# One layer of a hybrid encoder in one program: operands of the 512-column matmuls laid 256 bytes apart modulo 512 in SBUF

## The chip, the cores and the metric

The kernel runs on one core of one Trainium2 chip, as one program in one launch. The metric is device time in microseconds (us); the time before is the median of three runs, 946.27 us. The engines are named as in the profile: PE is TensorE's matmuls and PEld its loads of weights, DVE is VectorE, ACT is ScalarE, POOL is GpSimd and SP is SyncE, whose queue issues most of the DMAs. In this text a matmul's *stationary* operand is the one that PEld loads, and its *moving* operand the one that PE streams through; `pe.matmul(dst, a, b)` has `a` stationary and `b` moving. The *distance* of two operands is the difference of their byte addresses within a partition of SBUF, taken modulo 512.

## What is computed

One layer over 512 tokens of 1024 channels, in float32: a recurrent branch A and an attention branch B, merged by gates, and then a feed-forward block with a causal convolution. Both halves are normalised before and after.

```python
h = rms_norm(x, mix_norm_pre)
xa, ga, q, k, v, f, gA, gB = split(h @ w_in)
xc  = causal_conv4(xa)
y_a = gelu(ga) * rg_lru(xc, w_rg_a, w_rg_x, ...)      # 1280 channels
y_b = forgetting_attention(q, k, v, f + b_forget)     # 16 heads of 64
m   = sigmoid(gA) * (y_a @ w_proj_a) + sigmoid(gB) * (y_b @ w_proj_b)
x   = x + rms_norm(m @ w_out, mix_norm_post)
h   = rms_norm(x, ffn_norm_pre)
u   = causal_conv3(h @ w_up)                           # 6144 channels
x   = x + rms_norm((gelu(u_gate) * u_val) @ w_down, ffn_norm_post)
```

## The kernel before

**Three matmuls for one.** Each product is taken in three, to keep float32's precision in a faster format: an operand is split into a high part and a remainder (`hi` by ACT, `lo` by DVE; a tile of weights becomes `wh` and `wl`, activations `hh` and `hl`, `yh` and `yl`, `mh` and `ml`, `ah` and `al`), and `mm3` (L221) adds high by high, high by low and low by high into one bank of PSUM. `project` (L226) does that over the 8 blocks of 128 channels of k: 24 matmuls for one tile of 128 output channels by 512 tokens, each with its own load of 128 x 128 weights.

**The stages**, in the order in which TensorE runs them:

- xa: 10 tiles with the weights stationary and hh, hl moving. The first four (the *head*) run in halves of 256 tokens (`half`, L455): 192 matmuls of 256 columns. The other six, 144 matmuls of 512 columns, alternate with the recurrent gates (`gate_mm`, L371), whose stationary operand is `gh` or `gl` and whose moving one is xh, xl or a *halo* tile copied from the neighbours: 96 of 512 columns.
- v: 2 x 4 units; here hh, hl are stationary and the weights move (`v_mm`, L300): 192.
- ga: 10 tiles (240), then pa: 8 tiles over 10 blocks of k with yh, yl moving (240), and between them f, 16 small ones.
- The attention loop: for each of 8 pairs of heads q, k and ma by `project` (24 each), scores, the transposes `pt` of the probabilities P against `ident`, and `av`. Then mb and pb, 8 tiles each; in pb yb moves. So q, k, ma and mb have 768 matmuls of 512 columns together, pb 192.
- wo: mh, ml stationary, the weights moving (`out_matmuls`, L834): 192.
- up: the up-projection, all in matmuls of 256 columns with the weights stationary. Three pairs of tiles run plainly, in two halves of tokens (288); 21 pairs run in seven products of 12 (`Pair.product`, L901): 84 a pair, 1764 together. The remainders `ml` of some of their weights are made by an accumulating DMA on POOL's queue (L875).
- dn: the down-projection, 42 steps of 12 matmuls (`down_step`, L1198) with `ah`, `al` stationary and the weights moving: 504 of 512 columns. The `ah`, `al` of the first six steps lie in the pool `ff`, those of the others in `down`.

**Weights** come through one pool, `weights`, with tags `raw`, `wh` and `wl` of four buffers of 4096 bytes each. `unit` (L215) has them fetched two tiles ahead: a DMA on SP's queue into `raw`, ACT's copy to `wh`, DVE's subtraction to `wl`.

**Where tiles lie.** Pools are stacked from the left end of SBUF upwards or, with `side="right"`, from the right end downwards, in the order in which they are opened and closed; within a pool the tags follow one another in the order of their first use, each size rounded up to 32 bytes per partition. `offset(stack, n, side)` (L85) opens a pool of `n` bytes that nothing uses, so that what is opened behind it shifts by `n`. From the left there stand, in the kernel before: `consts` (a tile of 480 bytes that nothing uses, then 1952 bytes), `weights`, `small` (29 slots of 32 bytes), 160 bytes, hT (hh and hl), 320 bytes, vy0; on them `xc`, 448 bytes and `rgw` for the gates, later vy1, pa, tg and attn; and after these have gone, 96 bytes, x2, `norm` or `ff`, `up`, and at the end 256 bytes and `down`. From the right: 32 bytes; then 128 bytes and `rgate`; later h2T, 128 bytes and `merged`; and, when that is closed, `sums`, `tsum`, 448 bytes and `strassen`. The weights begin at 0 modulo 512, h2T at 448.

Of the kernel before, what the change touches and what calls it, by code (L numbers as in the profile page):

```python
# [8 lines left out]
F32 = mybir.dt.float32  # L9
# [7 lines left out]
P = 128  # L17
# [46 lines left out]
def kernel(  # L64
# [20 lines left out]
    def offset(stack, n, side="left"):  # L85

        places[0] += 1
        pool = stack.enter_context(tc.tile_pool(name=f"offset{places[0]}", bufs=1, side=side))
        pool.tile([P, n // 4], F32, name=f"offset{places[0]}")

    cpool = ctx.enter_context(tc.tile_pool(name="consts", bufs=1))
    cpool.tile([P, 120], F32, name="offset0")
    offset(ctx, 32, "right")
    wpool = ctx.enter_context(tc.tile_pool(name="weights", bufs=4))
    pstk = ctx.enter_context(ExitStack())
    pspools = [pstk.enter_context(tc.tile_pool(name="psum", bufs=8, space=PSUM, reuse_waits="tile"))]
    small = ctx.enter_context(tc.tile_pool(name="small", bufs=4))

    def bank(name):
        return pspools[-1].tile([P, 512], F32, tag="ps", name=name)  # L100
# [114 lines left out]
    def unit(name, ahead=2):  # L215

        i = where[name]
        fetch(i + ahead)
        return ready.pop(name)
# [6 lines left out]
    def project(dst, unit, ah, al, lo=0, hi=S):  # L226
        wh, wl = unit
        for k in range(KD):
            mm3(dst[:, lo:hi], wh[:, k], wl[:, k], ah[:, k, lo:hi], al[:, k, lo:hi], k == 0, k == KD - 1)
# [51 lines left out]

    mstk = ExitStack()
    gstk = ExitStack()
    offset(mstk, 160)
    hpool = mstk.enter_context(tc.tile_pool(name="hT", bufs=1))
    hh = hpool.tile([P, KD, S], F32R, name="hh")
    hl = hpool.tile([P, KD, S], F32R, name="hl")
    offset(mstk, 320)
    vpools = [mstk.enter_context(tc.tile_pool(name="vy0", bufs=4, reuse_waits="tile"))]
    vt, yb = {}, {}  # L290
    sp4 = cpool.tile([P, TR], F32, name="sp4")
# [27 lines left out]
    with ExitStack() as rg:  # L319
        rt, ixt, tt = {}, {}, {}  # L320
        last_act = [None]
        with ExitStack() as r0:
            xpool = r0.enter_context(tc.tile_pool(name="xc", bufs=6, reuse_waits="tile"))
            offset(r0, 448)
            gwpool = r0.enter_context(tc.tile_pool(name="rgw", bufs=2, reuse_waits="tile"))
            xc, xh, xl = {}, {}, {}

# [17 lines left out]
            def gate_prep(t):  # L345
                n = HROWS[t]
                raw = gwpool.tile([P, 4, P], F32, tag="graw", name=f"graw{t}")
                gh = gwpool.tile([P, 4, P], F32R, tag="gh", name=f"gh{t}")
                gl = gwpool.tile([P, 4, P], F32R, tag="gl", name=f"gl{t}")
                nc.sync.dma_start(raw, rgw[:, t])  # L350
                act.copy(gh, raw)
                stacked = 3 * n <= P
                hw = slice(0, 2 if stacked else 4)
                dve.tensor_tensor(out=gl[:, hw], in0=raw[:, hw], in1=gh[:, hw].bitcast(F32), op=ALU.subtract)
                th = gwpool.tile([P, S], F32R, tag="halo_h", name=f"halo_h{t}")
                tl = None
                if stacked:
                    q = slice(2 * n, 3 * n)
                    dve.tensor_tensor(out=gh[q, 2:4], in0=raw[q, 2:4], in1=gh[q, 2:4].bitcast(F32), op=ALU.subtract)
                    dsts = ((th, 0, xh), (th, n, xl), (th, 2 * n, xh))  # L360
                else:
                    tl = gwpool.tile([P, S], F32R, tag="halo_l", name=f"halo_l{t}", bufs=1)
                    dsts = ((th, 0, xh), (tl, 0, xl))
                for dst, o, src in dsts:
                    for c0, c1 in HALO[t]:
                        i = c0 // P
                        nc.sync.dma_start(dst[o : o + c1 - c0].bitcast(F32), src[i][c0 - i * P : c1 - i * P].bitcast(F32))
                        o += c1 - c0
                gw[t] = gh, gl, th, tl
# [22 lines left out]
            with tc.tile_pool(name="pre", bufs=2, side="right", reuse_waits="tile") as pre:  # L392
# [131 lines left out]
                split_a(2)  # L524
                fetch(NF + 1)
                gate_prep(0)
                conv_a(3, pss[3])
                split_a(3)

            offset(rg, 128, "right")  # L530
            rpool = rg.enter_context(tc.tile_pool(name="rgate", bufs=TR, side="right", reuse_waits="tile"))
            for t in range(NF, TR + NF):
                u = unit(order[t][0])
# [132 lines left out]
    def gate_tile(e, which):  # L666
        c = 0 if which == "ma" else KD
        pg = bank(f"{which}{e}")
        project(pg, unit(f"{which}{e}"), hh, hl)
        tg = tgpool.tile([P, S], F32, tag="tg", name=f"tg_{which}{e}")  # L670
        act.activation(out=tg, in_=pg, func=AF.Tanh, scale=0.5, bias=hb[:, c + e : c + e + 1])
        return tg

    with ExitStack() as at:
        apool = at.enter_context(tc.tile_pool(name="attn", bufs=2, reuse_waits="tile"))
# [8 lines left out]
        def prep_alloc(p):  # L684
            bias = []
            for h in (2 * p, 2 * p + 1):
                B = apool.tile([P, PO[NT]], F32, tag="B", name=f"B{h}")
                nc.gpsimd.dma_start(B, cnd[h : h + 1, :].partition_broadcast(P))
                for c0, w, o in ((0, 256, 0), (256, 512, 384)):
                    diag = B[:, c0 : c0 + 2 * w].rearrange("p (a b) -> p a b", a=2)[:, :, o : o + P]  # L690
                    nc.gpsimd.dma_start(diag, mask2, accum_op=ALU.add)  # L691
                bias.append(B)
            return bias

        def halves(ps, name):
            hi = apool.tile([P, S], F32R, tag=f"{name[0]}h", name=f"h_{name}")
            lo = apool.tile([P, S], F32R, tag=f"{name[0]}l", name=f"l_{name}")
            act.copy(hi, ps)
            dve.tensor_tensor(out=lo, in0=ps, in1=hi.bitcast(F32), op=ALU.subtract)
            return hi, lo  # L700
# [30 lines left out]
        def normalise(pts):  # L731
            for Pt, sm in pts:
                dve.reciprocal(sm, sm)
                for b in (3, 2, 0, 1):
                    w = P * (b + 1)
                    dve.tensor_scalar(out=Pt[:, PO[b] : PO[b] + w], in0=Pt[:, PO[b] : PO[b] + w],
                                      scalar1=sm[:, b : b + 1], scalar2=None, op0=ALU.mult)
# [45 lines left out]
        for p in range(KD):  # L783
            bias = prep_alloc(p)
            pq, pk = bank(f"q{p}"), bank(f"k{p}")
            project(pq, unit(f"q{p}"), hh, hl)
            if prev is not None:
                normalise(prev)
            project(pk, unit(f"k{p}"), hh, hl)
            q = halves(pq, f"q{p}")  # L790
            k = halves(pk, f"k{p}")
            if prev is not None:
                pts = pt(p - 1, prev)
            tg = gate_tile(p, "ma")
            dve.scalar_tensor_tensor(out=pa[:, p], in0=tg, scalar=1.0, in1=pa[:, p], op0=ALU.add, op1=ALU.mult)
            if prev is not None:
                av(p - 1, pts)
            prev = scores(p, q, k, bias)
# [8 lines left out]
    h2pool = ustk.enter_context(tc.tile_pool(name="h2T", bufs=1, side="right", reuse_waits="tile"))  # L807
    h2h = h2pool.tile([P, KD, S], F32R, name="h2h")
    h2l = h2pool.tile([P, KD, S], F32R, name="h2l")
    offset(gstk, 128, "right")  # L810
    mgpool = gstk.enter_context(tc.tile_pool(name="merged", bufs=1, side="right", reuse_waits="tile"))
    mh = mgpool.tile([P, KD, S], F32R, name="mh")
    ml = mgpool.tile([P, KD, S], F32R, name="ml")
# [13 lines left out]
    mstk.close()  # L827

    fstk = ctx.enter_context(ExitStack())
    offset(fstk, 96)  # L830
    xpool = fstk.enter_context(tc.tile_pool(name="x2", bufs=1, reuse_waits="tile"))
    x2t = xpool.tile([P, NT, D], F32, name="x2t")
    nc.sync.dma_start(x2t, xv)
# [100 lines left out]
    with ExitStack() as mix:  # L934
# [112 lines left out]
        for ps, u in first:  # L1047
            project(ps, u, h2h, h2l, 256, S)

    ypool = fstk.enter_context(tc.tile_pool(name="ff", bufs=3, reuse_waits="tile"))  # L1050
    ydram = ctx.enter_context(tc.tile_pool(name="ffd", bufs=1, space=bass.MemoryType.DRAM))
    yd = [ydram.tile([P, 2, S], F32, name=f"yd{j}") for j in range(JF // 2)]
# [86 lines left out]
    p, n = pairs[NU], pairs[NU + 1]  # L1139
# [85 lines left out]
    with man2:  # L1225
# [3 lines left out]
        b, p = pairs.pop(JF - 2), pairs.pop(JF - 1)  # L1229
# [45 lines left out]
        gelu(p.g)  # L1275
        glu(p.j, p.g, p.v)
        ustk.close()
        offset(fstk, 256)
        dpool = fstk.enter_context(tc.tile_pool(name="down", bufs=1, reuse_waits="tile"))
        dpools.append(dpool)  # L1280
        q = {}
# [207 lines left out]
```

## Time and profile before

| what | value |
|---|---|
| three runs | 944.2, 946.27, 946.84 us |
| profiled execution, span from the first to the last instruction | 941.1 us |
| granted clock of TensorE, mean | 0.998 |
| transposes `pt` of the attention loop | 256 by 226 ns, busy 10.7 us |
| DMA | 182.29 MB, mean 194 GB/s |
| POOL's `ml<-raw_up`, 512 KB | 20 DMAs, 5.5 us from issue to landing |

The profile is of one execution, apart from the timed runs; of it only the span is known, and the runs' median lies 5.2 us above that, for what comes ahead of the first instruction and behind the last. In the views of the profile a row of the windows gives, for a stretch of time, how long an engine was busy and how many of its instructions lie in the stretch in whole or in part. The duration of a matmul is longer than the time from its start to the start of the next, since matmuls are pipelined: rates are read from starts, or from counts over a stretch. The chain of waits follows the work that ended last back from the end; the view of the waits names, for each engine and line, what released it and how long it had stood.

### The profile page before, as it was taken

Reading aid. Unit: us, or ns where it says so; the run is one execution under the profiler, and the core shown is the slowest. Engines: PE = TensorE matmul, PEld = TensorE weight load, DVE = VectorE, ACT = ScalarE, POOL = GpSimd, SP = SyncE. Lnnn points to the kernel's source line nnn. Section 1 sums busy time; section 2 is a strip of 40 time slices with the busy share of each in tenths; the row PEclk is TensorE's granted clock in tenths of the full one; section 3 lists DMA queues with packets and bytes.
Section 4 is the critical chain, followed back from the end, with each engine's and each line's share of the span. In section 5 each row is a group of like instructions: output and inputs, shape, how many; then the busy total and the mean of one; then the engine's idle time right before and its main releaser. Section 6 shows DMA issues by size and latency. Waiting matters only on the chain.

```text
span 941.1 us, 14954 instructions
## 1 busy us (share of the span) xinstructions
PE 924.7 (98%) x5582; PEld 801.3 (85%) x5582; DVE 687.5 (73%) x1121; ACT 570.3 (61%) x982; POOL 228.6 (24%) x240
## 2 busy tenths in 40 slices
PE   9999999999999999999999999999999999999996
PEld 7888888887888888888888879999999999978885
DVE  5866369533757777777544488998888898889897
ACT  7554495333346666565322486687777878677664
POOL 4134335444243222220111000042322323100001
PEclk9999999999999999999999999999999999999999
DMA  7667589989686555552123753287898998799764
GB/s 276 227 212 209 155 224 277 248 194 254 174 227 151 152 151 149 157 154 70 68 90 103 282 187 123 57 233 184 201 214 211 207 219 207 217 367 335 235 207 143
DMA packets 76282, 182.29 MB, mean 194 GB/s; under 512 B 7281, under 2 KB 35745, under 8 KB 75826
## 3 DMA queue, kind: packets, MB, share of 16 engines
q1 hardware_dynamic: 45056, 123.13, 39.2%
q0 software_dynamic: 30864, 57.68, 29.9%
q8 instruction: 44, 0.72, 0.3%
q10 hardware_dynamic: 290, 0.53, 0.1%
q14 instruction: 28, 0.23, 0.1%
HBM read 148.59 MB, written 33.64 MB: 194 GB/s over the span
## 4 chain that ended last, share of the span: by engine, by line
PE 88%; DMA 5%; DVE 3%; ACT 2%; issue 1%; SPq 0%; DVEq 0%; ACTq 0%
PE up L915 5%; PE up L912 5%; PE up L913 5%; PE dn L1212 4%; PE dn L1210 4%; PE dn L1211 4%; DMA ml<-raw_up 4%; PE pa L224 2%; PE ga L224 2%; PE ga L223 2%; PE pa L223 2%; PE pa L222 2%; PE ga L222 2%; PE q L222 2%; PE ma L222 2%; PE wo L840 2%
## 5 line engine op out<-in xcount | busy, mean ns | idle before, releaser
L875 POOL DMA_DIRECT2D ml<-raw_up x41 | 36.5, 889 | 199.3 <-DVE ml L847 77.4
L1065 DVE SCALAR_TENSOR_TENSOR u<-up,cpt,u 128x511 f32<-128x511 f32 x96 | 71.3, 745 | 2.6 <-ACT u L1059 0.9
L1212 PE MATMUL dn<-wh_dn,al 128*128 128x512 f32 x168 | 65.6, 390 | 0.8 <-DVE al L847 0.8
L1210 PE MATMUL dn<-wh_dn,ah 128*128 128x512 f32 x168 | 65.4, 389 | 0.0
L1211 PE MATMUL dn<-wl_dn,ah 128*128 128x512 f32 x168 | 65.4, 389 | 0.0
L912 PE MATMUL up<-sh,th 128*128 128x256 f32 x252 | 61.8, 280 | 0.3 <-ACT x L919 0.3
L913 PE MATMUL up<-sl,th 128*128 128x256 f32 x252 | 61.6, 279 | 0.0
L175 DVE TENSOR_TENSOR wl_dn<-raw_dn,wh_dn 128x1024 fp32r<-128x1024 f32 x42 | 51.5, 1226 | 9.1 <-ACT wh_dn L172 8.9
L172 ACT CAST wh_dn<-raw_dn 128x1024 fp32r<-128x1024 f32 x42 | 44.1, 1050 | 17.3 <-issue 11.5
L847 DVE TENSOR_TENSOR tl<-t,th 128x1024 fp32r<-128x1024 f32 x42 | 51.1, 1217 | 1.8 <-ACT th L893 1.8
L1059 ACT ACTIVATE u<-up,cpt 128x512 f32<-128x512 f32 x48 | 37.0, 779 | 21.6 <-PE up L915 12.3
L893 ACT CAST th<-t 128x1024 fp32r<-128x1024 f32 x42 | 44.0, 1047 | 8.8 <-DVE t L847 6.1
L912 PEld LDWEIGHTS up<-sh,th 128*128 128x128 f32 x252 | 47.5, 188 | 0.7 <-ACT x L919 0.5
L913 PEld LDWEIGHTS up<-sl,th 128*128 128x128 f32 x252 | 47.5, 189 | 0.0
L691 POOL DMA_DIRECT2D B<-maskf x32 | 39.1, 1751 | 28.6 <-DMA B<-cnd 24.2
L1073 POOL TENSOR_TENSOR yf<-u,u 128x512 f32<-128x512 f32 x24 | 32.7, 1379 | 39.1 <-ACT u L1069 21.4
L912 PE MATMUL up<-h2h,mh 128*128 128x256 f32 x168 | 41.0, 279 | 0.0
L913 PE MATMUL up<-h2l,mh 128*128 128x256 f32 x168 | 41.0, 279 | 0.0
L931 DVE TENSOR_TENSOR up<-up,x 128x256 f32<-128x256 f32 x63 | 27.0, 432 | 17.9 <-PE up L915 9.4
L915 PE MATMUL up<-sh,tl 128*128 128x256 f32 x252 | 39.6, 279 | 0.0
L1212 PEld LDWEIGHTS dn<-wh_dn,al 128*128 128x128 f32 x168 | 31.5, 188 | 8.2 <-DVE al L847 1.6
L175 DVE TENSOR_TENSOR wl_pa<-raw_pa,wh_pa 128x640 fp32r<-128x640 f32 x16 | 13.1, 818 | 34.1 <-ACT wh_pa L172 34.1
(654 smaller groups left out, 3183.0 us busy)
## 6 DMA issues: line engine op xcount, KB each, us to landing
raw_up<-in_w_up_dram SPq DMA_DIRECT2D x48, 512.0 KB, 6.0
td<-in_w_down_dram POOLq DMA_DIRECT2D x36, 512.0 KB, 6.0
raw_dn<-td SPq DMA_DIRECT2D x24, 512.0 KB, 4.8
B<-cnd POOLq DMA_DIRECT2D x16, 640.0 KB, 5.2
ml<-raw_up POOLq DMA_DIRECT2D x20, 512.0 KB, 5.5
raw_dn<-in_w_down_dram SPq DMA_DIRECT2D x18, 512.0 KB, 4.2
raw_wo<-in_w_out_dram SPq DMA_DIRECT2D x16, 512.0 KB, 3.8
td<-td POOLq DMA_DIRECT2D x12, 512.0 KB, 10.7
```

Of the source, the lines that this page charges most:

```text
L172: act.copy(self.wh, self.raw)
L175: engine.tensor_tensor(out=self.wl, in0=self.raw, in1=self.wh.bitcast(F32), op=ALU.subtract)
L222: pe.matmul(dst, ah, bh, start=first, stop=False)
L847: dve.tensor_tensor(out=out, in0=a, in1=b, op=ALU.subtract)
L893: act.copy(self.th[i], self.t[i])
L912: pe.matmul(dst, wh[:, k], ah[:, k], start=first and k == 0, stop=False, skip_group_check=True)
L913: pe.matmul(dst, wh[:, k], al[:, k], start=False, stop=False, skip_group_check=True)
L915: pe.matmul(dst, wl[:, k], ah[:, k], start=False, stop=k == KH - 1, skip_group_check=True)
L1065: dve.scalar_tensor_tensor(out=c[:, s:], in0=ps[:, : S - s], scalar=col(C_CFW + 3 * e + j), in1=c[:, s:], op0=ALU.mult, op1=ALU.add)
L1210: pe.matmul(dst[t], ah[:, k, tok], wh[:, k], start=first, stop=False, skip_group_check=True)
L1211: pe.matmul(dst[t], ah[:, k, tok], wl[:, k], start=False, stop=False, skip_group_check=True)
L1212: pe.matmul(dst[t], al[:, k, tok], wh[:, k], start=False, stop=last, skip_group_check=True)
```

## The change

Only the places of tiles change: the sizes and the order of the tiles that are not used, and the place of the pool `small` ahead of the weights instead of behind them. Every instruction stays, in its order.

```diff
     cpool = ctx.enter_context(tc.tile_pool(name="consts", bufs=1))
-    cpool.tile([P, 120], F32, name="offset0")
     offset(ctx, 32, "right")
+    small = ctx.enter_context(tc.tile_pool(name="small", bufs=4))
+    offset(ctx, 64)
     wpool = ctx.enter_context(tc.tile_pool(name="weights", bufs=4))
     pstk = ctx.enter_context(ExitStack())
     pspools = [pstk.enter_context(tc.tile_pool(name="psum", bufs=8, space=PSUM, reuse_waits="tile"))]
-    small = ctx.enter_context(tc.tile_pool(name="small", bufs=4))
...
-    offset(mstk, 160)
+    offset(mstk, 256)
     hpool = mstk.enter_context(tc.tile_pool(name="hT", bufs=1))
     hh = hpool.tile([P, KD, S], F32R, name="hh")
     hl = hpool.tile([P, KD, S], F32R, name="hl")
-    offset(mstk, 320)
...
-            offset(r0, 448)
+            offset(r0, 256)
             gwpool = r0.enter_context(tc.tile_pool(name="rgw", bufs=2, reuse_waits="tile"))
...
+                if t == 0:
+                    gwpool.tile([P, 64], F32, name="offset_halo", bufs=1)
                 th = gwpool.tile([P, S], F32R, tag="halo_h", name=f"halo_h{t}")
...
-            offset(rg, 128, "right")
+            offset(rg, 192, "right")
             rpool = rg.enter_context(tc.tile_pool(name="rgate", bufs=TR, side="right", reuse_waits="tile"))
...
             q = halves(pq, f"q{p}")
+            if p == 0:
+                apool.tile([P, 64], F32, name="offset_k", bufs=1)
             k = halves(pk, f"k{p}")
...
-    offset(gstk, 128, "right")
+    offset(gstk, 192, "right")
     mgpool = gstk.enter_context(tc.tile_pool(name="merged", bufs=1, side="right", reuse_waits="tile"))
...
-    offset(fstk, 96)
     xpool = fstk.enter_context(tc.tile_pool(name="x2", bufs=1, reuse_waits="tile"))
...
+    offset(fstk, 256)
     ypool = fstk.enter_context(tc.tile_pool(name="ff", bufs=3, reuse_waits="tile"))
...
         ustk.close()
-        offset(fstk, 256)
         dpool = fstk.enter_context(tc.tile_pool(name="down", bufs=1, reuse_waits="tile"))
```

## The prediction

> **What bounds the kernel now.** The page comes first: the span, the busy times, the granted clock and the chain that ended last.
>
> ```profile
> span 941.1 us, 14954 instructions
> ## 1 busy us (share of the span) xinstructions
> PE 924.7 (98%) x5582; PEld 801.3 (85%) x5582; DVE 687.5 (73%) x1121; ACT 570.3 (61%) x982; POOL 228.6 (24%) x240
> ...
> PEclk9999999999999999999999999999999999999999
> ...
> PE 88%; DMA 5%; DVE 3%; ACT 2%; issue 1%; SPq 0%; DVEq 0%; ACTq 0%
> ```
>
> TensorE is busy for 98% of the span at full clock, and 88% of the chain is its own work. The view of the waits, for TensorE alone, says how little it is held up:
>
> ```profile
> PE up L915 <- DMA ml<-raw_up: 5.3, 6, 1.3
> PE xa L417 <- POOL ident masks.py:199: 1.5, 1, 1.5
> ```
>
> The longest sum is 5.3 us in six waits, all in the up-projection. So the time is the number of matmuls times the **spacing** of their starts, and a change of placement can act only through that spacing. The durations of the groups (some 390 ns for 512 columns) are no use here: matmuls overlap. I read the spacing from the view of windows instead. Each window below begins 0.20 us (0.06 us for 256 columns) after the start of one matmul and ends as long after the start of a later one of the same stage. With 512 columns one matmul is in flight at the left edge, so a row counting x has x-1 spacings; with 256 columns two are, so x-2. Columns: stretch, length, PE busy (count), clock, DMA share, GB/s.
>
> ```profile
> 25.16:30.81 5.65, 5.65 (x50) 1.00 0.31 100
> 112.22:131.81 19.59, 19.59 (x85) 1.00 0.51 142
> 150.26:188.94 38.68, 38.68 (x170) 1.00 1.07 257
> 194.20:223.96 29.76, 29.76 (x131) 1.00 1.04 221
> 258.10:267.48 9.38, 9.38 (x42) 1.00 0.92 256
> 460.18:467.39 7.21, 7.21 (x32) 1.00 0.30 98
> 526.27:549.83 23.56, 23.56 (x102) 1.00 0.62 216
> 668.09:676.25 8.16, 8.16 (x74) 1.00 0.90 222
> 718.51:816.03 97.52, 97.52 (x830) 1.00 0.89 215
> 823.86:829.07 5.21, 5.21 (x24) 1.00 0.98 322
> 838.08:877.75 39.67, 39.67 (x176) 1.00 0.96 339
> ```
>
> Every row is busy from edge to edge at clock 1.00, so nothing but the matmuls themselves sets these spacings. Beside each I put the distance of the stationary operand's address from the moving one's, modulo 512, worked out from the sizes of the pools in their order. The weights' tiles stand at 0 modulo 512. `small` is 29 slots of 32 bytes (928), plus 160 of offset, so hh and hl stand at 64; 320 more puts vy0, vy1, pa, tg and attn at 384. From the right, h2T stands at 448, and rgate and merged 128 lower at 320; `down` stands at 256, and the first six steps' `ah`, `al` in `ff` at 0.
>
> - v (row 112): stationary hh 64, moving weights 0: **64**; 19.59/84 = 233.2 ns
> - wo (526): stationary mh 320, moving weights 0: **320**; 23.56/101 = 233.3 ns
> - ga (150) and k, ma (258): weights 0, moving hh 64: **448**; 38.68/169 = 228.9 and 9.38/41 = 228.8 ns
> - pa (194): weights 0, moving yh 320: **192**; 29.76/130 = 228.9 ns
> - pb (460): weights 0, moving yb 384: **128**; 7.21/31 = 232.6 ns
> - dn (823): stationary ah 0, weights 0: **0**; 5.21/23 = 226.5 ns
> - dn (838): stationary ah 256, weights 0: **256**; 39.67/175 = 226.7 ns
>
> What the reader is to see: 64 and 320 agree, 448 and 192 agree, 0 and 256 agree, in stages that share nothing else (weights stationary in one, moving in the other; DMA share from 0.30 to 1.07). The spacing follows the distance modulo 256, and zero modulo 256 is the quickest shown. The 256-column rows are another matter: the head of xa (25.16, distance 448) has 5.65/48 = 117.7 ns, while the up-projection (64 throughout) has both 8.16/72 = 113.3 ns and 97.52/828 = 117.8 ns. It keeps a pattern over long stretches, and the chain of waits in order of time (start, length) shows what lies between some of them:
>
> ```profile
> 588.30:614.00 25.70, 25.70 (x220) 1.00 0.32 73
> 616.00:623.50 7.50, 7.41 (x63) 1.00 0.99 224
> 635.50:645.50 10.00, 9.00 (x80) 1.00 0.78 201
> 646.50:666.20 19.70, 19.18 (x163) 1.00 0.83 207
> 668.09:686.50 18.41, 17.62 (x156) 1.00 0.86 209
> 688.00:716.60 28.60, 27.45 (x243) 1.00 0.89 211
> 718.51:818.00 99.49, 99.49 (x840) 1.00 0.88 212
> ```
>
> ```profile
> 637.35 8.23 DMA ml<-raw_up
> ...
> 657.40 8.94 DMA ml<-raw_up
> ...
> 678.07 8.50 DMA ml<-raw_up
> ...
> 708.35 8.37 DMA ml<-raw_up
> ```
>
> Busy time by count is about 117.7 in the first, second, fourth and last stretch, about 113 in the others. The four transfers end at 645.6, 666.3, 686.6 and 716.7, where TensorE takes up again: it comes back slow, fast, fast and slow. So which pattern follows a wait is drawn there, and holds to the next.
>
> **The change, part by part.** No instruction is added, removed or moved; the tiles it adds (`offset_halo`, `offset_k`) are never touched. So all of it is distances. The new ones: `consts` loses 480 bytes and `small` moves ahead of the weights; 64 more brings the weights to 0 again. hT then starts 256 up, and with the 320 gone vy0, vy1, pa, tg and attn stand at 256 too. On the right 192 in place of 128 puts rgate and merged at 448-192 = 256. rgw starts at 0, its halo tiles at 256; `offset_k` leaves q at 256 and puts k, P and PTh at 0; `ff` and `down` stand at 256. So xa, v, ga, pa, q, k, ma, mb, pb, wo, gates, av and dn are all at 256, as the change says. f is not (its stationary slices step by 192 bytes), but has 16 matmuls. h2T and `sums` stay at 448 and their weights at 0: 64, as before.
>
> Counts are from the loops (8 blocks of k by 3 products a tile, 8 or 10 tiles). Savings, down to 226.7:
>
> - v, 192 by 233.2-226.7 = 6.5 ns: 1.25 us
> - wo, 192 by 6.6: 1.27 us
> - pb, 192 by 5.9: 1.13 us
> - ga and pa, 480 by 2.2: 1.06 us
> - q, k, ma, mb, 768 by 2.2: 1.69 us
> - xa after its head and the gates, 240 by 2.2: 0.53 us. Part of the gates (the halos) stands at zero already, and yet the stretch below, six matmuls from a halo to a halo, has 1.38/6 = 230 ns. I take it that a run of three does not settle; with distances equal throughout the stage the runs no longer break.
>
> ```profile
> 51.57:52.95 1.38, 1.38 (x7) 1.00 0.54 119
> ```
>
> - dn and av: 0 or 256 before, 256 after: nothing.
>
> That is 6.9 us. The **head of xa**, 192 matmuls of 256 columns, goes from 448 to 256, for which no row with 256 columns stands. Its bounds are 113.3 and 117.8 ns, the two patterns shown: 0.9 us to nothing. The 512-column row at the same distance is at its quickest, but v and the up-projection at 64 show that the two widths need not agree; I take the middle, 0.4 us.
>
> The **transposes** shift too: their stationary P goes from 288 to 384 (modulo 512) away from ident, which moves by 32 bytes. The groups by shape:
>
> ```profile
> L748 PE MATMUL pt<-ident,P 64*128 64x64 f32 x256 | 10.7, 226 | 0.0
> ...
> L257 PE MATMUL tr_f<-ident,xn 64*128 64x64 f32 x64 | 2.8, 229 | 0.0
> ```
>
> tr_f stands at 416, not 288, and has the same mean (229 and 226 ns): I cost them at nothing, 0.3 us either way.
>
> The **up-projection** keeps its distance, but its pattern is drawn anew after each wait, and every start ahead of it shifts. Slow in the rows above are 220+63+163+840 = 1286 of 2052 matmuls (288 and 21 pairs by 84). At 117.8-113.3 = 4.5 ns, all fast would be 5.8 us less; the other 766 at most all turned slow would be 3.4 us more. I take no change, with both ends for the range.
>
> Sum: 6.9 + 0.4 = 7.3 us, off a profiled span of 941.1: 933.8. The runs' median, 946.27, lies 5.2 us above that span for what is around it, so **939.0 us**. What TensorE gains in a stage it keeps, since the other engines follow it there, unless its weights come late. They do not now: a ga transfer lands in 5.2 us against 24 matmuls by 228.9 ns = 5.5 us a tile, two tiles are fetched ahead, and SP's queue waits there for a buffer that DVE frees, not for data.
>
> ```profile
> raw_ga<-in_w_in_dram SPq DMA_DIRECT2D x10, 512.0 KB, 5.2
> ```
>
> ```profile
> SPq L166 <- DVE wl_ga L175: 48.8, 10, 7.0
> ```
>
> If the cover went in ga and pa (DMA shares of 1.07 and 1.04), their 1.06 us would stay: 940.1.
>
> [...]
>
> **The rivals.**
>
> 1. *The up-projection settles in the slow pattern throughout.* For it: two of the four waits shown ended in it, the last, with 840 matmuls behind it, among them. Against: the fast one came back twice. 7.3 less 3.4 saved: 942.4.
> 2. *The change doesn't do what it says: placement is not the cause.* Then the two reads don't disturb each other, the spacings belong to the stages, and 512 columns stay as they are: 946.3. Against: three pairs of unlike stages agree by distance. [...]
> 3. *Slower: weights-stationary stages do not share dn's spacing.* Both rows at zero modulo 256 are dn, with an activation stationary and the weights moving. Direction does matter: 64 gives 233, and its negative 448 gives 229. If xa, gates, ga, pa, q, k, ma and mb (1488 matmuls) fell to 233.3 at 256, they would lose 1488 by 4.4 = 6.5 us, against 3.65 won in v, wo and pb: 949.2. It decides from 228.9 + 3650/1488 = 231.4 ns. Against: 256 is its own negative modulo 512, so the swap of roles leaves the distance as in dn.
>
> **How the numbers follow.** A measurement of this kernel tells from no change about 0.3%, 2.8 us, so "faster" means under 943.4. Forecast (226.7 ns at 512 columns, the up-projection mixed): 0.73. Rival 1: 0.14. Rival 2: 0.07. Rival 3: 0.04. The last 0.02 is a mishap of the new overlaps of tiles at a change of pools, worth a microsecond or two. Faster takes the forecast, rival 1 and a little: 0.88; same 0.08; slower 0.04. The range goes from 939.0-0.5 (head) less 5 of the 5.8 us of an all-fast up-projection, 933.5, to rival 1 with an unmoved head, 942.4+0.4 and 0.3 for the transposes: 943.1.
>
> **What would show it.** Right: windows over v, wo, pb, ga, pa and the attention's projections all at 226.7 ns, dn unchanged, PE's waits as before, and the rest of the difference in the stretches of the up-projection at 113.3 or 117.8. Wrong: a stage at 256 with another spacing than dn (rival 3, or 2 if it kept its old one); new waits of TensorE on a weight's DMA; an up-projection spacing outside the two patterns.

## The result and the profile after

The changed kernel takes 936.98 us in the median of 20 runs (932.72 to 942.19). The kernel before takes 943.5 us (939.87 to 948.82) in 20 runs, the three of the table above among them. The ratio is 0.9939, with a 95% interval of 0.9923 to 0.9954: 0.6% faster, twice the 0.3% that a measurement of this kernel can tell from no change. The profiled execution spans 934.0 us; its own time is 936.06, 2.1 us more. One later execution of the changed kernel took 4186 us, for a reason that was not looked into; it counts in the median of its experiment and in no ratio or mean.

From the page of the changed kernel (span, busy times, share of the chain):

```profile
span 934.0 us, 14955 instructions
...
PE 917.3 (98%) x5582; PEld 800.2 (86%) x5582; DVE 686.5 (74%) x1121; ACT 570.6 (61%) x982; POOL 230.2 (25%) x240
...
PE 91%; DMA 4%; DVE 2%; ACT 1%; issue 0%; DVEq 0%; POOL 0%; ACTq 0%; POOLq 0%
```

TensorE has the same 5582 matmuls in 7.4 us less. The windows over the changed kernel, laid as in the prediction (each begins 0.20 us after the start of a matmul and ends 0.20 us after that of a later one; 0.06 us for 256 columns; the spacing is the length divided by the count less one, or less two for 256 columns):

```profile
119.32:129.74 10.42, 10.42 (x47) 1.00 0.67 161
135.64:189.36 53.72, 53.72 (x238) 1.00 1.04 272
190.04:220.18 30.14, 30.14 (x134) 1.00 1.02 216
248.14:263.78 15.64, 15.64 (x70) 1.00 0.71 219
451.64:515.10 63.46, 63.46 (x281) 1.00 0.31 103
516.92:549.33 32.41, 32.41 (x144) 1.00 0.65 229
835.02:870.16 35.14, 35.14 (x156) 1.00 0.96 332
...
19.99:27.18 7.19, 7.19 (x62) 1.00 0.62 219
690.07:730.65 40.58, 40.58 (x360) 1.00 0.85 210
747.55:807.62 60.07, 60.07 (x512) 1.00 0.87 221
```

The first seven rows are v, ga, pa, the first pair's q, k and ma, the second phase's pb and mb, wo, and dn. They give 226.5, 226.7, 226.6, 226.7, 226.6, 226.6 and 226.7 ns: each of these 512-column stages now has dn's spacing, whichever operand stands still and whether the DMA share is 0.31 or 1.04. The eighth row, the head of xa, has 7.19/60 = 119.8 ns where it had 117.7: with 256 columns the new distance is *slower*. The last two are the up-projection, in its quick pattern (40.58/358 = 113.4 ns) and its slow one (60.07/510 = 117.8 ns), both still there.

The view of TensorE's waits:

```profile
PE up L917 <- DMA ml<-raw_up: 6.4, 6, 2.0
PE xa L418 <- POOL ident masks.py:199: 1.5, 1, 1.5
PE dn L1215 <- DVE al L849: 0.8, 1, 0.8
```

Only the first differs in a way that matters: 6.4 us for 5.3. Its longest wait, 2.0 us at 626, has an aftermath. From the timeline of TensorE, and then from the windows around it:

```profile
628.32 0.92 PE L917 MATMUL up<-h2h,ml 128*128 128x256 f32 x4 [2.02 <-DMA ml<-raw_up]
```

```profile
622.50:626.00 3.50, 3.50 (x32) 1.00 1.03 255
626.10:628.20 2.10, 0.20 (x2) 1.00 0.83 178
628.40:631.90 3.50, 3.50 (x18) 0.54 0.43 62
632.20:640.00 7.80, 7.80 (x71) 1.00 0.89 244
```

For 3.5 us after the wait the granted clock is 0.54, and 18 matmuls stand where 32 stood just before. At some 206 ns instead of 115, the 17 spacings cost another 1.5 us. A wait of 2 us here costs 3.5.

Where the 7.1 us between the two spans come from, by the start times of equal matmuls in the two traces: 0.8 us have been gained by the gates at 42 us (TensorE's waits there for xn, hl and a halo, of 0.2, 0.3 and 0.4 us, stand in the profile of before alone; it will turn out to be chance), 6.7 more by the end of wo, 0.5 in the up-projection (250.8 to 250.3 us), and 0.9 are lost after it (120.8 to 121.7 us).

### The profile page after: what moved, and what is told of

It reads as the page before. It is cut to its first block, busy times and chain, and to the rows that moved or that the text cites. A ratio compares the mean times of both kernels' runs of the same rounds, so it can differ in the third digit from the quotient of the medians.

```text
span 934.0 us, 14955 instructions
## 1 busy us (share of the span) xinstructions
PE 917.3 (98%) x5582; PEld 800.2 (86%) x5582; DVE 686.5 (74%) x1121; ACT 570.6 (61%) x982; POOL 230.2 (25%) x240
## 4 chain that ended last, share of the span: by engine, by line
PE 91%; DMA 4%; DVE 2%; ACT 1%; issue 0%; DVEq 0%; POOL 0%; ACTq 0%; POOLq 0%
PE up L917 6%; PE up L914 5%; PE up L915 5%; PE dn L1215 4%; PE dn L1213 4%; PE dn L1214 4%; DMA ml<-raw_up 4%; PE pa L223 2%; PE ga L224 2%; PE ga L223 2%; PE pa L224 2%; PE pa L222 2%; PE ga L222 2%; PE ma L222 2%; PE q L222 2%; PE wo L842 2%
## 5 line engine op out<-in xcount | busy, mean ns | idle before, releaser
L1213 PEld LDWEIGHTS dn<-wh_dn,ah 128*128 128x128 f32 x168 | 31.5, 188 | 6.7 <-ACT ah L1187 0.5
```

The lines of the kernel that those rows point to most:

```text
L1213: pe.matmul(dst[t], ah[:, k, tok], wh[:, k], start=first, stop=False, skip_group_check=True)
```

## The experiments

The theory: the spacing of settled matmuls is set by the distance of the stationary from the moving address, modulo 256, by a curve of its own for each width; at 512 columns zero is best, at 256 columns it isn't; and the up-projection's pattern is drawn by the moment at which TensorE comes back from a wait. The rivals: the period is 512; the spacing belongs to the stage; the up-projection's pattern has a cause other than its distance and the moment.

**A sweep of distances by itself.** A kernel of its own: matmuls on zeros in the order of `project`, nothing else running; it computes nothing of the layer. Its core, with e set by the distance:

```
for k in range(KD):
    ...                                       # b: block k of the weights; c: n columns, from e into block k of hh
    pe.matmul(dst, wh[:, b], hh[:, c], ...)
    pe.matmul(dst, wh[:, b], hl[:, c], ...)
    pe.matmul(dst, wl[:, b], hh[:, c], ...)
```

> A kernel of its own: x is copied to the output, and beside it runs of matmuls on zeros in project's order (wh by hh, wh by hl, wl by hh over 8 blocks of k), 48 of 512 columns or 72 of 256 columns each, at distances 0, 32, ... 480 between stationary and moving operand, every run begun by a short wait for DVE (2 runs a distance with 512 columns, 6 with 256). It computes nothing of the layer. Theory (the spacing of settled matmuls is set by the distance modulo 256): 512 columns give 226.7 ns at 0 and 256, about 233 at 64 and 320, 232.6 at 128 and 384, 228.9 at 192 and 448; 256 columns give 113.3 or 117.8 at 64 and 320, 117.8 at 192 and 448 and, like the changed kernel's head, 119 to 120 at 0 and 256. Rival (the stage sets its spacing, not the distance): one spacing for all distances. Rival (period 512): the pairs 256 apart differ. The other distances are unknown; one with 256 columns at 113.3 in all six runs would be a better place for the up-projection.

Windows over it, 36 spacings each for 512 columns (distance 0, 64, 128, 192, 256, 320), then 48 for 256 columns (distance 0 and 64):

```profile
24.02:32.18 8.16, 8.16 (x37) 1.00 0.01 2
68.57:76.97 8.40, 8.40 (x37) 1.00 0.00 0
113.40:121.77 8.37, 8.37 (x37) 1.00 0.01 2
157.94:166.18 8.24, 8.24 (x37) 1.00 0.00 0
202.21:210.37 8.16, 8.16 (x37) 1.00 0.01 2
246.76:255.16 8.40, 8.40 (x37) 1.00 0.00 0
412.82:418.58 5.76, 5.76 (x50) 1.00 0.00 0
514.94:520.59 5.65, 5.65 (x50) 1.00 0.00 0
```

That is 226.7, 233.3, 232.5, 228.9, 226.7 and 233.3 ns, then 120.0 and 117.7. The layer's values for 0, 64, 128 and 192 come back to 0.2 ns with next to nothing else running (DMA share 0.01): the spacing belongs to the distance, not to the stage. The whole curve, in ns, from the starts in the trace (the same at every distance plus 256, to 0.2 ns):

| distance | 0 | 32 | 64 | 96 | 128 | 160 | 192 | 224 |
|---|---|---|---|---|---|---|---|---|
| 512 columns | 226.7 | 233.3 | 233.3 | 234.2 | 232.5 | 233.3 | 228.9 | 233.3 |
| 256 columns | 120.0 | 118.3 | 117.8 | 118.7 | 118.7 | 120.0 | 117.8 | 116.7 |

So the period is 256, and the two widths have different best places: zero is the best of the row at 512 columns and, with 160, the worst at 256. All six runs of 64 with 256 columns came out at 117.8; the quick pattern did not show.

**All 512-column stages at distance 0 instead of 256.** The changed kernel with its spacers set so that the operands stand 0 apart modulo 512, not 256:

```diff
-    offset(mstk, 256)
...
-            offset(r0, 256)
...
-            offset(rg, 192, "right")
+            offset(rg, 448, "right")
...
-    offset(gstk, 192, "right")
+    offset(gstk, 448, "right")
...
-    offset(fstk, 256)
```

(the spacers `offset_halo` and `offset_k` go too)

> The changed kernel with all its 512-column stages at distance 0 instead of 256. Theory (period 256): v, wo, ga, pa, pb, dn and the attention's projections stay at 226.7 ns each, time within what the up-projection's patterns move it (931 to 942 us). Rival (256 modulo 512 is special, two operands at the same place in 512 disturb each other most): spacings of 230 to 241 ns in those stages, 7 to 30 us more.

One execution: 940.39 us, beside 943.69 for the kernel before. Its v, in a window, has 20.40/90 = 226.7 ns:

```profile
119.24:139.64 20.40, 20.40 (x91) 1.00 0.75 183
```

Over all its unstalled 512-column matmuls, what lies above 226.7 ns sums to 1.2 us, as in the changed kernel (1.2; 7.9 before). A period of 512 with its best at 256 is out. The total is above the changed kernel's median for a reason ahead of these stages: at the start of v this execution stands 4.2 us behind the changed kernel's profile, after a wait of 1.8 us in the gates, in whose wake seven matmuls of xa have spacings of 430 ns instead of 227. The up-projection, with a wait of 3.8 us, took 251.2 us, 0.8 more than in that profile. The two waits:

```profile
PE up L911 <- DMA ml<-raw_up: 5.2, 4, 3.8
PE gate L375 <- DMA halo_h<-xl: 1.8, 1, 1.8
```

**The up-projection at 256 as well.** The changed kernel with h2T and `sums` moved too:

```diff
+    offset(ustk, 192, "right")
...
     h2h = h2pool.tile([P, KD, S], F32R, name="h2h")
...
-    offset(gstk, 192, "right")
...
-    offset(ustk, 448, "right")
+    offset(ustk, 256, "right")
```

> The changed kernel with the up-projection at 256 as well (h2T, sums moved; its weights stay). Theory (the head of xa, 256 columns at 256, stands for it: 119 to 120 ns): 2052 matmuls by 119.5 less a mean near 115 ns: 9 us more, no 113.3 pattern anywhere. Rival (256 columns follow 512 columns, with zero the quickest): 113.3 throughout, 3 to 4 us less than the changed kernel.

One execution: 943.02 us beside 943.69 for the kernel before, so nearly the whole gain is gone. A window over its up-projection has 31.08/259 = 120.0 ns, and its waits are fewer:

```profile
702.94:734.02 31.08, 31.08 (x261) 1.00 0.80 206
```

```profile
PE up L917 <- DMA ml<-raw_up: 3.6, 4, 1.1
```

The stage takes 256.8 us, 6.5 more than in the changed kernel. The matmuls alone would make it some 10 us (1261 quick ones by 6.7 ns and 752 slow ones by 2.2); the rest is made up by shorter waits for `ml<-raw_up` (3.6 us for 6.4): none of them, 1.1 us at most, was followed by a stretch at half clock as the wait of 2.0 us above was, and the mean granted clock is 0.999 where that profile has 0.996. Whether the slower pace is what shortened the waits isn't shown. It was right not to move this stage to 256 with the others, and its time isn't the sum of its spacings.

**One stage alone.** The kernel before with wo's `merged` moved from 320 to 256, and nothing else:

```diff
-    offset(gstk, 128, "right")
+    offset(gstk, 192, "right")
```

> The kernel before with one number changed: merged at 256 instead of 320, so wo's distance alone goes from 320 to 256. Theory (each stage goes by its own distance): wo falls from 233.3 to 226.7 ns, 1.27 us; v stays at 233.2, ga and pa at 228.9, pb at 232.6. Rival (the spacings go with the lay-out as a whole): wo stays near 233, or others move with it.

Windows over v and wo:

```profile
121.25:131.98 10.73, 10.73 (x47) 1.00 0.70 168
523.18:555.61 32.43, 32.43 (x144) 1.00 0.65 229
```

wo has gone to 32.43/143 = 226.8 ns, 1.2 us less in all, and v has stayed at 10.73/46 = 233.3. The up-projection starts 1.2 us earlier than before (568.0 to 566.8 us after the first matmul). Of these two stages only the one whose distance changed has another spacing. And yet this run took 945.91 us, 2.2 more than the kernel before beside it:

```profile
PE up L915 <- DMA ml<-raw_up: 7.9, 6, 2.2
```

Two of these waits, at 632 and 745, were followed by stretches at half clock (0.994 in the mean of the execution, 0.998 in the profile of before), and the up-projection took 254.7 us where the profiled kernel before has 250.8. A gain of 1.2 us ahead of it can't be seen through what it does from one execution to the next.

**Finer distances, and when the pattern is drawn.** A second kernel of its own, on zeros, computing nothing of the layer: distances between those of the sweep, stationaries that alternate between two places, and the up-projection's order of products with 256 columns, ten runs for each of 16 distances, begun by different waits: two for the first stationary, two for the first moving operand, and six for a stationary in the middle of the first product, behind other work of different lengths.

> A kernel of its own like m1, nothing of the layer is computed. First 512 columns in project's order at the distances 4, 8, 16, 48, ... 240, 248, 252 (one run of 48 each), then runs of 48 at moving distance 0 in which every second stationary stands 64, 128 or 192 bytes off. Then 256 columns in the order of the up-projection's products (6 products of 12) at 0, 16, ... 240, ten runs a distance that differ only in the wait ahead: the first load waits (2), the first moving operand waits (2), or a load in the middle of the first product waits for DVE, behind 0 to 960 columns of other DVE work (6). Theory (the pattern of the up-projection is drawn by the exact moment at which the matmuls take up again): at 64 both 113.3 and 117.8 ns come up among the ten, at 192 only 117.8, at 0 only 120. Rival (an order or a kind of wait decides): at 64 each kind has one spacing. In m1, where every run began with a wait of the first load, 64 gave 117.8 six times of six. If one distance gives 113.3 in all ten, the up-projection belongs there. With 512 columns no distance but 0 modulo 256 is expected at 226.7; if the load that counts is the next matmul's, then in the alternating runs the long spacing stands at the matmul ahead of the shifted load.

With 512 columns I had expected no distance but zero to give 226.7 ns; of those added here 16 does. 4, 8 and 252 have 230.7, 232.3 and 237.7. With the stationaries 128 apart in turn, so that one of the two stands at zero, a window over 36 spacings has 8.40/36 = 233.3 ns:

```profile
168.87:177.27 8.40, 8.40 (x37) 1.00 0.01 2
```

Half the matmuls at the best distance bring nothing where the other half are 128 off; where they are 64 or 192 off, the mean is 230.0. At 64 it splits into 231.5 after the shifted stationary's matmul and 228.5 after the other's; I had expected the load of the next stationary to be what disturbs, which would have put the longer one elsewhere, so what makes the difference stays open.

With 256 columns, windows over 42 spacings each: distance 64 begun by a wait for the stationary and by one of the waits for the moving operand, then distance 144 in the same two cases:

```profile
543.83:548.59 4.76, 4.76 (x44) 1.00 0.00 0
560.89:565.84 4.95, 4.95 (x44) 1.00 0.02 3
972.47:977.23 4.76, 4.76 (x44) 1.00 0.01 3
989.47:994.23 4.76, 4.76 (x44) 1.00 0.02 3
```

At 64 both patterns exist without the rest of the layer: 113.3 ns in three runs, 117.9 in seven. The two runs begun by a wait for the moving operand came out one either way, and they differ only in the length of the copy that they waited for: there the moment of the start was enough to decide. The kind of wait may count too, for both runs begun by the first stationary were quick and all six begun in the middle of a product slow. At 144 all ten runs settle at 113.3, which no other of the 16 distances does.

**The changed kernel once more**, beside the kernel of the next experiment.

> The changed kernel again, on the same chip and in the same rounds as e5. Its 512-column stages at 226.7 ns, its up-projection mixed anew of 113.3 and 117.8 ns; ratio to the kernel before 0.991 to 0.996.

935.34 us in the median of seven runs (933.19 to 944.9), the kernel before 941.55; ratio 0.993 (0.9904 to 0.9956). Its profiled execution is the 944.9. By the matmuls' starts it had lost 2.7 us to the first profile at 42 us already, and the stages from there to the up-projection took the same time. The up-projection took 257.0 us with *more* quick spacings than the first profile (1631 to 1261), because it waited more (and two of these waits, at 641 and 784, were followed by matmuls at about half speed: a matmul's record is 0.28 us long ahead of the second, 2.8 us long, and 0.41 us behind it):

```profile
PE up L917 <- DMA ml<-raw_up: 11.7, 8, 2.8
```

**The up-projection at 144.** The changed kernel with h2T and `sums` each as one tile whose data begin 16 bytes in, so that the distance can be 144, with the same instructions on every engine:

```diff
+    offset(ustk, 64, "right")
...
-    h2h = h2pool.tile([P, KD, S], F32R, name="h2h")
-    h2l = h2pool.tile([P, KD, S], F32R, name="h2l")
-    offset(gstk, 192, "right")
+    h2 = h2pool.tile([P, 4 + 2 * KD * S], F32R, name="h2")
+    h2h, h2l = (h2[:, 4 + i * KD * S : 4 + (i + 1) * KD * S].rearrange("p (k s) -> p k s", k=KD) for i in range(2))
+    offset(gstk, 96, "right")
...
+        offset(ustk, 224, "right")
...
+        sums = spool.tile([P, 4 + 8 * KH * SH], F32R, name="sums")
...
-    offset(ustk, 448, "right")
+    offset(ustk, 96, "right")
```

> The changed kernel with the up-projection at 144 instead of 64 (modulo 256), the instructions the same. Theory (the distance sets the pattern, and m2 had 113.3 in ten of ten runs at 144): all 2052 matmuls at 113.3 ns, none at 117.8, whatever the waits; the stage, 250.3 us in the changed kernel's profile, comes to 2052 by 113.3 = 232.5 us and the waits for ml, which were 8.2 us at 702 fast matmuls and 10.2 at 1261 and so should be 12 to 15 us now: 245 to 248 us. So 2 to 5 us less than the changed kernel, 930 to 934 us by its median, with a smaller spread from run to run. Rival (the waits set the pace of the stage): the spacing falls and the waits take all of it, no difference. Rival (m2's short runs on zeros don't carry over): 117.8 or another spacing in parts.

934.63 us in the median of six runs (931.34 to 937.32), just above the 930 to 934 expected; ratio to the kernel before 0.9925 (0.9899 to 0.995). Windows over its up-projection have 31.06/274 = 113.4 and 29.24/258 = 113.3 ns, and its waits are no longer than the changed kernel's:

```profile
670.23:701.29 31.06, 31.06 (x276) 1.00 0.88 219
776.27:805.51 29.24, 29.24 (x260) 1.00 0.87 237
```

```profile
PE up L918 <- DMA ml<-raw_up: 5.4, 5, 1.8
```

The stage takes 245.9 us, with some 1912 quick spacings and 113 of 116 to 124 ns, nearly all of them among the first dozen after a wait or a late start. But the interval holds the changed kernel's 0.993.

**Both again**, on one chip, the changed kernel and then the one at 144.

> The changed kernel once more, beside e7. Median 934 to 938 us, ratio 0.991 to 0.996.

> e5's kernel once more, to tell whether it is quicker than the changed kernel. Theory (quick pattern throughout, waits as in the profile of e5, 8.6 us): median 1 to 3 us below the changed kernel's of the same rounds, and a spread of some 6 us against some 10. Rival (waits for ml grow as the matmuls get quicker): medians within 1 us of one another.

The changed kernel: 938.59 us, 0.6 above the range expected, ratio 0.9954 (0.9929 to 0.9979). At 144: 934.47 us, ratio 0.9938 (0.9916 to 0.9959), 4.1 us less than the changed kernel where 1 to 3 were expected. The stage took 250.9 us in the one profile and 245.8 in the other. Their waits:

```profile
PE up L917 <- DMA ml<-raw_up: 8.7, 7, 2.5
```

```profile
PE up L918 <- DMA ml<-raw_up: 5.2, 7, 1.1
```

So the waits did not grow as the matmuls got quicker: both profiles at 144 wait less (5.4 and 5.2 us) than any of the three of the changed kernel (6.4, 11.7 and 8.7). The intervals of the ratios still meet. Over all measurements the changed kernel has a mean of 937.3 us in 38 runs (standard deviation 2.8) and the one at 144 a mean of 934.9 in 13 (2.1): 2.4 us less, with an uncertainty of 2 times the root of 2.8²/38 + 2.1²/13, 1.5 us. The first 20 of the 38 were measured without the one at 144 beside them; the other 18 alone have a mean of 937.5, 2.6 us more than at 144, with an uncertainty of 2.0. The kernel at 144 is the quicker of the two by these pooled means, though the intervals of the two ratios don't show it.

## Why the prediction was right, and where it was off

**Right: the mechanism and its size.** The terms, as predicted and as summed from the starts in the two traces:

| term | predicted us | measured us |
|---|---|---|
| v | 1.25 | 1.20 |
| wo | 1.27 | 1.19 |
| pb | 1.13 | 1.06 |
| ga and pa | 1.06 | 1.09 |
| q, k, ma, mb | 1.69 | 1.51 |
| xa after its head, gates | 0.53 | 0.48 |
| sum | 6.9 | 6.5 |

All but ga and pa are a little low. The gates still hold 0.34 us above 226.7 ns by each matmul, and ma 0.29: there short runs stand between other matmuls, which was not shown to be the cause. dn is unchanged, as is the cover: but for `ml<-raw_up`, which stood there before, no weight's DMA appears among TensorE's waits. The attention loop's transposes held nothing to speak of: their spacings sum to 9.9 us in both traces. From the gates at 42 us to the end of wo the two traces part by 6.7 us, 0.2 from the sum of the terms.

**Mis-sized: the head of xa.** The prediction bounded it by the two patterns of the up-projection, 113.3 and 117.8 ns, and took the middle, a gain of 0.4 us. It went outside these bounds, to 119.8 ns: 192 by 2.1 ns, a loss of 0.4 us. Two values at one distance were taken as the ends for another. The sweep shows 120.0 at zero with 256 columns and 116.7 to 120.0 over its distances, so the warning that the two widths need not agree should have moved the value, not just stood beside it.

**Mis-sized: the way from the span to the median.** "The runs' median, 946.27, lies 5.2 us above that span" took a property of three runs for one of the kernel. What lies around a span is 2.1 us (936.06 to 934.0); the other 3 us were that those three runs were long: the median of twenty is 943.5. The span came out at 934.0 where 933.8 was worked out, and the median at 936.98 where 939.0 was. Nearly all of that error is this step; between the two medians of twenty lie 6.5 us, where 7.3 was forecast.

That the span came out within 0.2 us is luck. The terms came 0.4 us short of the forecast and the head 0.8; the up-projection brought 0.5 that was not forecast, and chance (below) some 1.2 at the start less 0.9 at the end. The two further profiles of the same kernel span 942.9 and 936.7 us.

**No change in the up-projection: right in sum, by two things that cancel.** In the profiled pair the quick spacings went from 702 to 1261, worth 2.5 us by 4.5 ns each. The time above the two patterns went from 8.2 to 10.2 us, the half-clock stretch included, so 0.5 us was left: luck as well. The prediction counted the pattern alone; the stage is also held by its transfers, for which TensorE waits here and there from 600 us on (5.3 and 6.4 us in the pair). The three profiles of the changed kernel have 1261, 1631 and 1819 quick spacings, and stages of 250.3, 257.0 and 250.9 us: in the two later ones the time above the patterns, 18.6 and 13.3 us for 10.2, outweighs what more quick spacings save. That time does not simply grow with the pace: the two profiles at 144, quick nearly throughout, have 8.7 and 8.6 us. What sets the lengths of these waits stays open. Nor does a pattern always hold to the next wait, as the prediction had it: in the changed kernel it turned at 738.4 us without one (below).

**The chance parts of the profiled difference.** The 0.8 us gained by 42 us (with the head's loss in it) is not the change's: two further profiles of the changed kernel stand 2.7 and 2.6 us later there than its first. The 0.9 us lost after the up-projection is of the same kind: that stretch takes 120.8 us before and 121.0 to 122.1 in the profiles of the experiments. I did not trace either to one wait.

**The rivals.** The first, an up-projection slow throughout, did not come: 752 of its spacings were slow, 1326 before. The second, that placement isn't the cause, is out by the sweep, where the distance alone moves the spacing by 7.5 ns, from 226.7 to 234.2 at one clock, with next to nothing else running. The third, that stages with stationary weights don't share dn's spacing, is out by 226.7 ns in ga and 226.6 in pa.

## What to carry to other kernels

Where TensorE is busy to the edge, read the spacing of starts in windows, not the durations, and compare it between stages of equal width: stages that differ only in where their operands lie show what placement costs (here 226.7 to 233.3 ns for 512 columns). A best distance found at one width must be measured again at another; here zero modulo 256 is the best of the sweep for 512 columns and, with 120.0 ns, among the worst for 256. In these runs a gain ahead of a stage that waits on its own transfers shows over many executions (medians of twenty, 943.5 and 936.98 us) and was lost in a single one (wo's 1.2 us, in an execution 2.2 us longer than that of the kernel before), so judge a microsecond by the stage's windows and not by the total of one run.

## What the hardware showed besides

- **Two patterns at one distance.** With 256 columns at 64 the same matmuls run at 113.3 or 117.8 ns, and keep to one of them for hundreds of matmuls (510 spacings in the row from 747.55). Which one can be decided by the moment of the start: in the second kernel on zeros two runs that differ only in the length of the copy they waited for have 113.3 and 117.9. In the changed kernel a weight load some 20 ns late at 738.4 (135 ns behind the one before it, in a row of 113) went ahead of the turn from quick to slow. At 144 only the quick one was seen.
- **Half clock after a short wait.** Of the ten longest waits in the up-projections of the nine profiles of the layer, 1.8 to 3.8 us of idle time each, seven were followed by 11 to 17 matmuls at about half speed; none of the others from 0.8 us up was. The granted clock was 0.54 behind the 2.0 us (row above), and 0.50 behind 2.4 us in the third profile of the changed kernel. Two waits of 1.8 us were followed by it, and three of 1.8, 1.9 and 2.5 us were not. What decides between them was not tried.
- **The curve is not smooth.** At 512 columns 16 is as good as zero (226.7 ns), and 4 bytes short of zero, 252, is the worst of all (237.7).
